# Weight sums in another order, and a chunk's last gate behind the next chunk's first PSUM copy, in a four-layer trunk on one core

## The chip, the core and the metric

The kernel runs on one core of a Trainium2 chip. The metric is the device time of one execution in microseconds (us), as the median of several runs. The engines are TensorE (PE in the profile; PEld is its weight load), VectorE (DVE), ScalarE (ACT), GpSimd (POOL) and SyncE (SP, which issues the loads). Each takes its own instructions in order, and waits at an instruction until all that it needs is there.

## The reference, cut to what matters

A trunk of four layers over 256 rows of width 1024, all in fp32. Each layer is a feed-forward block (FFN), an attention (of one of three kinds) and another FFN, so there are eight FFNs. The change lies in the FFN alone.

```python
D_MODEL, SEQ, DEPTH, D_FF = 1024, 256, 4, 2816

def swiglu(x, w_in, w_out):
    gate, up = jnp.split(x @ w_in, 2, axis=-1)
    return (jax.nn.silu(gate) * up) @ w_out

for i in range(DEPTH):
    h = h + 0.5 * rms_norm(swiglu(rms_norm(h, g[0]), ffn_w_in[i, 0], ffn_w_out[i, 0]), g[1])
    m = ...  # one of three attentions of rms_norm(h, g[2])
    h = h + rms_norm(m, g[3])
    h = h + 0.5 * rms_norm(swiglu(rms_norm(h, g[4]), ffn_w_in[i, 1], ffn_w_out[i, 1]), g[5])
```

## The kernel before

**Products.** An fp32 product is made of three products of fp32r parts. Every weight unit of 1 MB (a "raw" tile of 128 x 2048) is split into hi, cast by ScalarE (L156), and lo = raw − hi, by VectorE (L157). A group for one unit is then 12 matmuls of 128x512 (L152): four steps of k, each hi·xh, lo·xh, hi·xl. At most RAWS = 9 raw buffers and UNITS = 4 split units are held at a time in an FFN, and the names b00, b01, ... below are such units.

**An FFN** goes over D_FF in six chunks: chunk 0 is 512 wide, chunk 1 is 256 wide, chunks 2 to 5 are 512 wide. Chunks 0 and 1 are "plain" (function plain): gate and up for the two row tiles of 128, one after the other. Chunks 2 to 5 are in WINO (function wino): the eight products of the gate and the up of two row tiles, each in two halves of k, are made from seven, after Winograd. With b00, b01 the gate's and the up's upper half of k, and b10, b11 the lower, the weights of the seven are b00, b10, t2 = b00 + b01 + b11, t1 = b00 + b01, t3 = b01 + b11, b11, and t4 = t2 + b10 in this order. The left sides are rows of x, or sums of them (sh, sl in the profile).

**Where the sums are made.** plan_wino lists the loads and the splits ("preps") of a chunk, and fill works them off while there are raw buffers and split slots free. After the split of b00, VectorE adds b01 to b00 (L372): that is t1. After the split of b10, VectorE makes t2 = t1 + b11 in a buffer of its own (L372), and a DMA issued by GpSimd adds b11 to b01 (L375): t3. After the split of t2, another such DMA adds b10 to t2 (L375): t4. So there are two VectorE sums and two adding DMAs in a chunk, 64 of each in the kernel.

**Through a chunk.** wino(j) fills PSUM bank pb with b00, copies it to sl0 on ScalarE (L487), transposes the gate of the chunk before for row tile 0 (turn, tpg, L434; the transposed gate is split to gh and gl with L156 and L157), fills bank pa with b10, adds it to sl0 (L482) and takes the silu (L493), transposes the gate for row tile 1, and adds t2 on top of b00 in pb. That is why the copy of pb must be over first. Then the chunk before goes through its down projection in pieces (y, L244 to L246), with the products of t1, t3, b11 and t4 in between. The two gates of a chunk are made with up (L426) on VectorE: gate 0 after b11, gate 1 at the end, after t4's product has been added to sl1 (L482) and sl1 has gone through the silu (L518).

**What sets the order.** The code only says in which order the work is written; a scheduler of the language then sets each engine's list from it, once, when the kernel is built. The numbered names in the lists below are the built program's: g01_3_1 is the gate of layer 0, FFN 1, chunk 3, row tile 1, and raw423 or lo446 are the numbers of a raw tile or a split unit.

Of the kernel before, what the change touches and what calls it, by code (L numbers as in the profile page):

```python
# [11 lines left out]
AF = mybir.ActivationFunctionType  # L12
ALU = mybir.AluOpType
# [33 lines left out]
class Trunk:  # L47
# [235 lines left out]
    def ffn(self, l, f, X, ahead, end):  # L283
        nc = self.nc
        with self.tc.tile_pool(name=f"ffn{l}{f}", bufs=2, reuse_waits="tile") as pool:
# [73 lines left out]
            def plan_wino(j):  # L359


                c0, w = chunks[j]
                name = lambda n: (j, n)
                quarter = lambda k, u: (w_in, k * 512, 4, u * D_FF + c0, w)
                c1, w1 = chunks[j - 1]
                ko = [((j - 1, "o", k), (w_out, c1 + k * P, 2, 0, D)) for k in range(0, w1 // P, 2)]
                for n, src in ((name("b00"), quarter(0, 0)), (name("b01"), quarter(0, 1)),
                               (name("b10"), quarter(1, 0)), (name("b11"), quarter(1, 1)), (name("t2"), None), *ko):
                    loads.append(lambda n=n, src=src: raw(n, src))

                def add(to, a, b):
                    nc.vector.tensor_tensor(R[name(to)], R[name(a)], R[name(b)], op=ALU.add)  # L372

                def add_by_dma(to, b):
                    nc.gpsimd.dma_start(R[name(to)], R[name(b)], accum_op=ALU.add)  # L375

                def quarters(n, then=()):
                    split(name(n), name(n))
                    for x in then:
                        (add if len(x) == 3 else add_by_dma)(*x)  # L380

                def last_of(n, of, gone=None):
                    split(name(n), name(of), True)
                    if gone:
                        free(name(gone))

                outs = [lambda n=n: split(n, n, True) for n, _ in ko]
                preps.extend([
                    lambda: quarters("b00", [("b00", "b00", "b01")]),
                    lambda: quarters("b10", [("t2", "b00", "b11"), ("b01", "b11")]),  # L390
                    lambda: quarters("t2", [("t2", "b10")]),
                    outs[0],
                    lambda: last_of("t1", "b00"),
                    lambda: last_of("t3", "b01"),
                    lambda: last_of("b11", "b11")])
                if j < last:
                    preps.extend(outs[1:])
                preps.append(lambda: last_of("t4", "t2", "b10"))
                if j == last:
                    preps.extend(outs[1:])  # L400

# [8 lines left out]
            def unit(n):  # L410
                fill()
                return U[n]
# [57 lines left out]
            def wino(j):  # L470
# [16 lines left out]
                nc.scalar.copy(sl0, B)  # L487
                fill()
# [12 lines left out]
                o(1, 0)  # L501
                times(B, s31, 4, "t1", False)
# [14 lines left out]
                add(sl1, C)  # L517
                nc.scalar.activation(sl1, sl1, AF.Silu, scale=X[1][1])  # L518
                up(1, g1, 512, sl1, j, nr[1], g1)
                fill()  # L520
                if j < last:
                    del G[j - 1, 0], G[j - 1, 1]

# [19 lines left out]
            zig = [(0, 0), (0, 1), (1, 0), (1, 1)]  # L543
            for j in range(1, last + 1):
                if j in WINO:
                    wino(j)
                    continue
                plain(j, zig, [lambda: turn(j - 1, 0), lambda: turn(j - 1, 1)])
# [5 lines left out]
                del G[j - 1, 0], G[j - 1, 1]  # L554
            turn(last, 0)
# [770 lines left out]
```

## Time and profile before

| | us |
|---|---|
| median of 3 runs | 2004.0 (2003.55 to 2004.16) |
| the profiled execution | 2004.23 |
| its span in the profile | 2002.3 |
| TensorE busy | 1932.5 (97%) |
| VectorE busy | 1609.4 (80%) |
| ScalarE busy | 1257.2 (63%) |
| GpSimd busy | 188.6 (9%) |

The profile is of one execution; times in its views count from the span's start. TensorE's granted clock was 0.998 of full speed on average. A row of a timeline says when an instruction started, how long it took, its engine, line and operation, the tiles that it writes and reads, and, in square brackets, how long the engine had been idle before it and what ended that. A matmul's duration is longer than the distance to the next one, since they are pipelined.

### The profile page before, as it was taken

The numbers are of one execution on the slowest core, as the hardware profiler recorded it, in microseconds if no ns is written. First come the engines' busy times: TensorE is split into PE (matmuls) and PEld (weight loads), VectorE is DVE, ScalarE is ACT, GpSimd is POOL, SyncE is SP. The second block draws the span as 40 slices with busy tenths as digits, with TensorE's granted clock in tenths as the row PEclk, the third lists the DMA queues.
The fourth block names the chain that finished last, engine by engine and source line by source line (L and its number), as shares of the span: only waits on it lengthen the run. The fifth ranks groups of instructions, "written<-read, shape, count | busy, mean of one in ns | idle before, by whom it ended". The sixth has DMA issues, their size and how long they took to land.

```text
span 2002.3 us, 25733 instructions
## 1 busy us (share of the span) xinstructions
PE 1932.5 (97%) x9712; PEld 1584.9 (79%) x9712; DVE 1609.4 (80%) x2040; ACT 1257.2 (63%) x1721; POOL 188.6 (9%) x303
## 2 busy tenths in 40 slices
PE   7999999999999999999999999999999999999998
PEld 6777878777877878877887787678778777878776
DVE  6888678888788766788879877877988888678886
ACT  6566666566566566566656666865666657576654
POOL 0001210000000120000000032000000000210000
PEclk9999999999999999999999999999999999999999
DMA  9795638696787556687877675166868785638782
GB/s 360 213 295 140 211 120 294 184 294 188 245 274 222 169 189 212 184 278 211 283 221 212 209 205 165 60 242 200 230 208 300 202 286 148 206 105 286 203 286 55
DMA packets 177867, 430.25 MB, mean 215 GB/s; under 512 B 8784, under 2 KB 37712, under 8 KB 169552
## 3 DMA queue, kind: packets, MB, share of 16 engines
q1 hardware_dynamic: 168528, 361.51, 50.7%
q0 software_dynamic: 9216, 67.11, 17.6%
q8 instruction: 76, 1.25, 0.2%
q14 instruction: 47, 0.39, 0.1%
HBM read 360.43 MB, written 1.05 MB: 181 GB/s over the span
## 4 chain that ended last, share of the span: by engine, by line
PE 79%; ACT 8%; DVE 7%; issue 3%; POOL 0%; ACTq 0%; DVEq 0%; POOLq 0%
PE ps L152 13%; PE pb L152 12%; PE y L246 9%; PE y L244 9%; PE y L245 9%; PE pc L152 6%; ACT hi L156 5%; PE pa L152 4%; PE pw L670 4%; PE pw L672 4%; PE pw L671 3%; DVE lo L157 3%; DVE raw L372 2%; PE tpg L434 1%; ACT gh L156 1%
## 5 line engine op out<-in xcount | busy, mean ns | idle before, releaser
L157 DVE TENSOR_TENSOR lo<-raw,hi 128x2048 fp32r<-128x2048 f32 (+3 forms) x534 | 984.7, 1861 | 251.3 <-ACT hi L156 250.8
L156 ACT CAST hi<-raw 128x2048 fp32r<-128x2048 f32 (+3 forms) x534 | 824.8, 1563 | 481.6 <-DVE raw L372 189.9
L244 PE MATMUL y<-hi,gh 128*128 128x512 f32 x704 | 277.6, 394 | 5.1 <-ACT gh L156 5.1
L245 PE MATMUL y<-lo,gh 128*128 128x512 f32 x704 | 275.2, 391 | 0.0
L246 PE MATMUL y<-hi,gl 128*128 128x512 f32 x704 | 265.7, 391 | 0.0
L152 PE MATMUL ps<-hi,xh 128*128 128x256 f32 (+1 forms) x512 | 175.4, 342 | 1.9 <-ACT xh L156 1.3
L152 PE MATMUL pb<-hi,sh 128*128 128x512 f32 x384 | 153.1, 399 | 21.1 <-ACT sl L487 21.1
L152 PE MATMUL ps<-lo,xh 128*128 128x256 f32 (+1 forms) x512 | 173.2, 338 | 0.2 <-DVE lo L157 0.2
L152 PE MATMUL ps<-hi,xl 128*128 128x256 f32 (+1 forms) x512 | 172.9, 338 | 0.0
L244 PEld LDWEIGHTS y<-hi,gh 128*128 128x128 f32 x704 | 132.2, 188 | 41.7 <-ACT gh L156 15.2
L670 PE MATMUL pw<-hi,xh 128*128 128x512 f32 (+2 forms) x432 | 164.6, 381 | 0.0
L672 PE MATMUL pw<-hi,xl 128*128 128x512 f32 (+2 forms) x432 | 155.9, 361 | 0.0
L671 PE MATMUL pw<-lo,xh 128*128 128x512 f32 (+2 forms) x432 | 155.4, 360 | 0.0
L246 PEld LDWEIGHTS y<-hi,gl 128*128 128x128 f32 x704 | 132.2, 188 | 27.4
L375 POOL DMA_DIRECT2D raw<-raw x64 | 55.5, 868 | 1037.6 <-DVE raw L372 644.3
L245 PEld LDWEIGHTS y<-lo,gh 128*128 128x128 f32 x704 | 132.3, 188 | 26.0
L152 PE MATMUL pb<-lo,sh 128*128 128x512 f32 x384 | 151.8, 395 | 0.0
L152 PE MATMUL pb<-hi,sl 128*128 128x512 f32 x384 | 149.5, 389 | 0.0
L372 DVE TENSOR_TENSOR raw<-raw,raw 128x2048 f32<-128x2048 f32 x64 | 146.0, 2282 | 0.0
L152 PEld LDWEIGHTS ps<-hi,xh 128*128 128x128 f32 x512 | 97.6, 191 | 13.2 <-ACT xh L156 2.2
L152 PEld LDWEIGHTS pb<-hi,sh 128*128 128x128 f32 x384 | 72.0, 188 | 45.3 <-ACT sl L487 31.2
L152 PEld LDWEIGHTS ps<-lo,xh 128*128 128x128 f32 x512 | 97.6, 191 | 11.2 <-DVE lo L157 1.1
(213 smaller groups left out, 3327.2 us busy)
## 6 DMA issues: line engine op xcount, KB each, us to landing
raw<-in_ffn_w_in SPq DMA_DIRECT2D x172, 1024.0 KB, 8.4
raw<-in_ffn_w_out SPq DMA_DIRECT2D x88, 1024.0 KB, 9.2
raw<-raw POOLq DMA_DIRECT2D x64, 1024.0 KB, 7.0
raw<-in_diff_w_in SPq DMA_DIRECT2D x24, 1024.0 KB, 5.2
raw<-in_moba_w_in SPq DMA_DIRECT2D x12, 1024.0 KB, 5.2
raw<-in_nsa_w_in SPq DMA_DIRECT2D x9, 1024.0 KB, 5.1
raw<-in_diff_w_out SPq DMA_DIRECT2D x8, 1024.0 KB, 4.9
gpre<-in_norm_g SPq DMA_DIRECT2D x12, 512.0 KB, 5.9
```

The lines of the kernel that those rows point to most:

```text
L152: nc.tensor.matmul(out, l, r, start=first and i == 0, stop=last and i == len(steps) - 1, skip_group_check=more)
L156: self.nc.scalar.copy(hi, src)
L157: self.nc.vector.tensor_tensor(lo, src, hi.bitcast(F32), op=ALU.subtract)
L244: nc.tensor.matmul(y[b], x[0][:, kt, :], hi[:, k, s], start=f, stop=False)
L245: nc.tensor.matmul(y[b], x[0][:, kt, :], lo[:, k, s], start=False, stop=False)
L246: nc.tensor.matmul(y[b], x[1][:, kt, :], hi[:, k, s], start=False, stop=l)
L372: nc.vector.tensor_tensor(R[name(to)], R[name(a)], R[name(b)], op=ALU.add)
L375: nc.gpsimd.dma_start(R[name(to)], R[name(b)], accum_op=ALU.add)
L434: nc.tensor.transpose(tp[:, k, :], g[:, k * P:(k + 1) * P], self.ident)
L670: nc.tensor.matmul(out, x[0][:, kt, :], hi[:, k, :], start=first and i == 0, stop=False)
L671: nc.tensor.matmul(out, x[0][:, kt, :], lo[:, k, :], start=False, stop=False)
L672: nc.tensor.matmul(out, x[1][:, kt, :], hi[:, k, :], start=False, stop=last and i == len(todo) - 1)
```

## The change

In wino chunks the weight sums are made in another order:

- t1 gets a buffer of its own. t1 = b00 + b01 is a VectorE sum (L406), and b01 += b11, which is t3, an adding DMA (L407). Both stand in a new function sums_of(j + 1), which is called one chunk ahead: in wino(j) after the first down-projection pieces, for chunk 2 inside plain(1). It first takes loads off the list until t1 has its buffer.
- In the chunk itself, after the split of b10, VectorE adds b01 to b00 (L374). As b01 is b01 + b11 by then, that is t2. After the split of t2 the adding DMA b00 += b10 makes t4 (L378).
- The loads are listed as b00, b01, b11, (t1's buffer), b10, then the units of the down projection. In the last chunk the remaining units of the down projection still come after t4.
- The number of sums, adding DMAs, loads, splits and products is as before.

The last gate of a chunk (the add to sl1, the silu and up) becomes a function gate1 that wino returns. It is called in the next chunk's wino, behind the copy of pb to sl0, and after the last chunk at the end. unit calls fill only where the unit isn't there yet.

```diff
-                for n, src in ((name("b00"), quarter(0, 0)), (name("b01"), quarter(0, 1)),
-                               (name("b10"), quarter(1, 0)), (name("b11"), quarter(1, 1)), (name("t2"), None), *ko):
+                for n, src in ((name("b00"), quarter(0, 0)), (name("b01"), quarter(0, 1)), (name("b11"), quarter(1, 1)),
+                               (name("t1"), None), (name("b10"), quarter(1, 0)), *ko):
                     loads.append(lambda n=n, src=src: raw(n, src))
...
+                def sum_t2():
+                    split(name("b10"), name("b10"))
+                    nc.vector.tensor_tensor(R[name("b00")], R[name("b00")], R[name("b01")], op=ALU.add)
+
+                def split_t2():
+                    split(name("t2"), name("b00"))
+                    nc.gpsimd.dma_start(R[name("b00")], R[name("b10")], accum_op=ALU.add)
+
+                def split_t4():
+                    split(name("t4"), name("b00"), True)
+                    free(name("b10"))
 
                 outs = [lambda n=n: split(n, n, True) for n, _ in ko]
                 preps.extend([
-                    lambda: quarters("b00", [("b00", "b00", "b01")]),
-                    lambda: quarters("b10", [("t2", "b00", "b11"), ("b01", "b11")]),
-                    lambda: quarters("t2", [("t2", "b10")]),
+                    lambda: split(name("b00"), name("b00")),
+                    sum_t2,
+                    split_t2,
                     outs[0],
-                    lambda: last_of("t1", "b00"),
-                    lambda: last_of("t3", "b01"),
-                    lambda: last_of("b11", "b11")])
+                    lambda: split(name("t1"), name("t1"), True),
+                    lambda: split(name("t3"), name("b01"), True),
+                    lambda: split(name("b11"), name("b11"), True)])
...
+            def sums_of(j):
+
+                if j not in WINO:
+                    return
+                while (j, "t1") not in R:
+                    loads.pop(0)()
+                b01 = R[j, "b01"]
+                nc.vector.tensor_tensor(R[j, "t1"], R[j, "b00"], b01, op=ALU.add)
+                nc.gpsimd.dma_start(b01, R[j, "b11"], accum_op=ALU.add)
...
             def unit(n):
-                fill()
+                if n not in U:
+                    fill()
                 return U[n]
...
                 nc.scalar.copy(sl0, B)
+                gate1()
                 fill()
                 turn(j - 1, 0)
...
                 o(0, 0)
                 o(1, 0)
+                sums_of(j + 1)
                 times(B, s31, 4, "t1", False)
...
                 times(C, X[1][0], 4, "t4", False)
-                add(sl1, C)
-                nc.scalar.activation(sl1, sl1, AF.Silu, scale=X[1][1])
-                up(1, g1, 512, sl1, j, nr[1], g1)
-                fill()
+
+                def gate1():
+                    add(sl1, C)
+                    nc.scalar.activation(sl1, sl1, AF.Silu, scale=X[1][1])
+                    up(1, g1, 512, sl1, j, nr[1], g1)
                 if j < last:
                     del G[j - 1, 0], G[j - 1, 1]
+                return gate1
...
-                plain(j, zig, [lambda: turn(j - 1, 0), lambda: turn(j - 1, 1)])
+                plain(j, zig, [lambda: turn(j - 1, 0), lambda: turn(j - 1, 1), lambda: sums_of(j + 1)])
...
+            gate1()
+            fill()
             turn(last, 0)
```

**In the built lists.** First VectorE at the end of chunk 3 of the second FFN. Before: lo445 is the split of chunk 4's b00, lo446 that of its b10, lo447 that of its t2.

```order
L157 TENSOR_TENSOR lo445_3579<-raw423_3350,hi445_3578 128x2048
L426 SCALAR_TENSOR_TENSOR g01_3_0_3595<-pb431_3433,st396_3004,sl01_3_0_3446 128x512
L372 TENSOR_TENSOR raw423_3350<-raw423_3350,raw424_3352 128x2048
L157 TENSOR_TENSOR lo446_3598<-raw430_3431,hi446_3597 128x2048
L372 TENSOR_TENSOR raw436_3482<-raw423_3350,raw433_3452 128x2048
L482 TENSOR_TENSOR sl01_3_1_3504<-pc444_3564,sl01_3_1_3504 128x512
L157 TENSOR_TENSOR lo447_3628<-raw436_3482,hi447_3627 128x2048
L426 SCALAR_TENSOR_TENSOR g01_3_1_3554<-g01_3_1_3554,st397_3006,sl01_3_1_3504 128x512
```

After, with the rows ahead of it (lo437, lo439 and lo441 are splits of chunk 3's b11, of an output unit and of t4; g01_3_1 at L490 is the add of a product to the last gate's up part):

```order
L157 TENSOR_TENSOR lo437_3507<-raw402_3045,hi437_3506 128x2048
L406 TENSOR_TENSOR raw433_3452<-raw423_3350,raw424_3352 128x2048
L157 TENSOR_TENSOR lo439_3537<-raw421_3320,hi439_3536 128x2048
L157 TENSOR_TENSOR lo441_3559<-raw395_2990,hi441_3558 128x2048
L490 TENSOR_TENSOR g01_3_1_3556<-pc444_3566,g01_3_1_3556 128x512
L157 TENSOR_TENSOR lo445_3581<-raw423_3350,hi445_3580 128x2048
L434 SCALAR_TENSOR_TENSOR g01_3_0_3596<-pb429_3424,st396_3004,sl01_3_0_3437 128x512
L157 TENSOR_TENSOR lo446_3599<-raw436_3481,hi446_3598 128x2048
L374 TENSOR_TENSOR raw423_3350<-raw423_3350,raw424_3352 128x2048
L490 TENSOR_TENSOR sl01_3_1_3504<-pc444_3566,sl01_3_1_3504 128x512
L157 TENSOR_TENSOR lo447_3628<-raw423_3350,hi447_3627 128x2048
L434 SCALAR_TENSOR_TENSOR g01_3_1_3556<-g01_3_1_3556,st397_3006,sl01_3_1_3504 128x512
```

One sum (L406) now stands three splits, an add and a gate earlier, and between the two gates there are two splits and one sum instead of two splits and two sums.

Second, ScalarE in the same stretch. Before: hi447 is the cast of t2, L518 the last gate's silu, hi448 and hi451 the casts of an output unit and of chunk 4's t1, L487 the copy of pb.

```order
L156 CAST hi447_3627<-raw436_3482 128x2048
L518 ACTIVATE sl01_3_1_3504<-sl01_3_1_3504,st368_2826 128x512
L156 CAST hi448_3647<-raw438_3510 128x2048
L487 COPY sl01_4_0_3666<-pb450_3653 128x512
L156 CAST hi451_3668<-raw423_3350 128x2048
L156 CAST gh01_3_0_3679<-tpg01_3_0_3674 128x512
```

After:

```order
L156 CAST hi447_3627<-raw423_3350 128x2048
L530 ACTIVATE sl01_3_1_3504<-sl01_3_1_3504,st368_2826 128x512
L495 COPY sl01_4_0_3657<-pb448_3644 128x512
L156 CAST hi449_3662<-raw438_3510 128x2048
L156 CAST hi451_3668<-raw433_3452 128x2048
L156 CAST gh01_3_0_3678<-tpg01_3_0_3673 128x512
```

The copy stands one cast earlier; the cast of t2 and the silu are still ahead of it.

Third, VectorE at the end of chunk 2. Before: lo422 is the split of chunk 2's t4, lo425 and lo427 those of chunk 3's b00 and b10.

```order
L157 TENSOR_TENSOR lo422_3347<-raw386_2881,hi422_3346 128x2048
L157 TENSOR_TENSOR lo425_3369<-raw395_2990,hi425_3368 128x2048
L482 TENSOR_TENSOR g01_2_1_3366<-pc426_3373,g01_2_1_3366 128x512
L372 TENSOR_TENSOR raw395_2990<-raw395_2990,raw400_3039 128x2048
L157 TENSOR_TENSOR lo427_3388<-raw402_3045,hi427_3387 128x2048
L372 TENSOR_TENSOR raw416_3266<-raw395_2990,raw413_3245 128x2048
L426 SCALAR_TENSOR_TENSOR g01_2_0_3405<-pb414_3247,st396_3004,sl01_2_0_3260 128x512
L482 TENSOR_TENSOR sl01_2_1_3314<-pc426_3373,sl01_2_1_3314 128x512
```

After (raw413, the buffer of chunk 3's t1, takes the place in memory that raw378, which lo422 reads, leaves):

```order
L157 TENSOR_TENSOR lo422_3347<-raw378_2849,hi422_3346 128x2048
L406 TENSOR_TENSOR raw413_3245<-raw395_2990,raw400_3039 128x2048
L157 TENSOR_TENSOR lo425_3371<-raw395_2990,hi425_3370 128x2048
L490 TENSOR_TENSOR g01_2_1_3368<-pc426_3374,g01_2_1_3368 128x512
L157 TENSOR_TENSOR lo427_3389<-raw416_3265,hi427_3388 128x2048
L434 SCALAR_TENSOR_TENSOR g01_2_0_3405<-pb414_3246,st396_3004,sl01_2_0_3259 128x512
L374 TENSOR_TENSOR raw395_2990<-raw395_2990,raw400_3039 128x2048
L490 TENSOR_TENSOR sl01_2_1_3314<-pc426_3374,sl01_2_1_3314 128x512
```

The sum for t1 stands one split and one add ahead of where it was, right behind the split of chunk 2's t4, and gate 0 now stands ahead of the sum that makes t2.

## Rows read from the trace of the kernel before

**Rows 1.** The page's head: the span, and each engine's busy time

```profile
span 2002.3 us, 25733 instructions
...
PE 1932.5 (97%) x9712; PEld 1584.9 (79%) x9712; DVE 1609.4 (80%) x2040; ACT 1257.2 (63%) x1721; POOL 188.6 (9%) x303
```

**Rows 2.** TensorE's waits: line, releaser; us in total, times, longest us

```profile
PE pb L152 <- ACT sl L487: 21.1, 24, 0.9
PE tpg L434 <- DVE g L426: 14.1, 8, 1.8
...
PE y L244 <- ACT gh L156: 5.1, 24, 0.2
...
PE ps L152 <- DVE lo L157: 0.2, 1, 0.2
```

**Rows 3.** Timeline of TensorE, chunk 3 to 4: start us, us, instruction [idle before]

```profile
423.63 0.39 PE L152 MATMUL pb<-lo,xh 128*128 128x512 f32 x1
423.86 0.40 PE L152 MATMUL pb<-hi,xl 128*128 128x512 f32 x1
...
427.05 0.39 PE L152 MATMUL pa<-hi,xl 128*128 128x512 f32 x1
428.34 0.51 PE L152 MATMUL pb<-hi,sh 128*128 128x512 f32 x1 [0.90 <-ACT sl L487]
...
432.33 0.39 PE L245 MATMUL y<-lo,gh 128*128 128x512 f32 x1
432.93 0.50 PE L244 MATMUL y<-hi,gh 128*128 128x512 f32 x1 [0.21 <-ACT gh L156]
```

**Rows 4.** Timeline of ScalarE in the passages 2 to 3 and 3 to 4

```profile
395.18 0.57 ACT L487 COPY sl<-pb 128x512 f32<-128x512 f32 x1
...
423.49 1.90 ACT L156 CAST hi<-raw 128x2048 fp32r<-128x2048 f32 x1 [8.16 <-DVE raw L372]
425.30 0.72 ACT L518 ACTIVATE sl<-sl,st 128x512 f32<-128x512 f32 x1
425.92 1.89 ACT L156 CAST hi<-raw 128x2048 fp32r<-128x2048 f32 x1
427.71 0.57 ACT L487 COPY sl<-pb 128x512 f32<-128x512 f32 x1
```

**Rows 5.** Timeline of VectorE, chunk 3 to 4

```profile
408.82 2.29 DVE L157 TENSOR_TENSOR lo<-raw,hi 128x2048 fp32r<-128x2048 f32 x1 [2.39 <-ACT hi L156]
...
416.03 0.74 DVE L426 SCALAR_TENSOR_TENSOR g<-pb,st,sl 128x512 f32<-128x512 f32 x1
...
418.89 2.28 DVE L157 TENSOR_TENSOR lo<-raw,hi 128x2048 fp32r<-128x2048 f32 x1
...
425.42 2.29 DVE L157 TENSOR_TENSOR lo<-raw,hi 128x2048 fp32r<-128x2048 f32 x1 [1.44 <-ACT hi L156]
427.63 0.75 DVE L426 SCALAR_TENSOR_TENSOR g<-g,st,sl 128x512 f32<-128x512 f32 x1
```

**Rows 6.** Timeline of VectorE, chunk 2 to 3

```profile
378.18 2.29 DVE L157 TENSOR_TENSOR lo<-raw,hi 128x2048 fp32r<-128x2048 f32 x1 [2.29 <-ACT hi L156]
381.34 2.29 DVE L157 TENSOR_TENSOR lo<-raw,hi 128x2048 fp32r<-128x2048 f32 x1 [0.87 <-ACT hi L156]
...
384.15 2.28 DVE L372 TENSOR_TENSOR raw<-raw,raw 128x2048 f32<-128x2048 f32 x1
...
390.75 0.74 DVE L426 SCALAR_TENSOR_TENSOR g<-pb,st,sl 128x512 f32<-128x512 f32 x1
```

**Rows 7.** Timeline of TensorE, chunk 2 to 3

```profile
391.55 0.66 PE L434 MATMUL tpg<-ident,g 128*128 128x128 f32 x4 [1.76 <-DVE g L426]
...
399.09 0.39 PE L244 MATMUL y<-hi,gh 128*128 128x512 f32 x1
```

**Rows 8.** The adding DMAs of L375: one issue on GpSimd, and all landings

```profile
386.79 0.85 POOL L375 DMA_DIRECT2D raw<-raw  x1 [21.94 <-DVE raw L372]
...
DMA to landing us min/median/max: 6.9/7.0/9.7
```

More of the change, by code (lines that the diff above doesn't have):

```diff
@@ L369, in plan_wino @@
                     loads.append(lambda n=n, src=src: raw(n, src))
[L371 to L385, printed above, removed]
+                def sum_t2():
[4 more added lines that the diff above has]
+                    nc.gpsimd.dma_start(R[name("b00")], R[name("b10")], accum_op=ALU.add)
@@ L392, in plan_wino @@
                     outs[0],
-                    lambda: last_of("t1", "b00"),
-                    lambda: last_of("t3", "b01"),
-                    lambda: last_of("b11", "b11")])
+                    lambda: split(name("t1"), name("t1"), True),
+                    lambda: split(name("t3"), name("b01"), True),
+                    lambda: split(name("b11"), name("b11"), True)])
                 if j < last:
                     preps.extend(outs[1:])
-                preps.append(lambda: last_of("t4", "t2", "b10"))
+                preps.append(split_t4)
@@ L468, in plain, with wino @@
                         between.pop(0)()
-            def wino(j):
+            def wino(j, gate1):
                 def times(ps, x, at, n, first):
@@ L543, in ffn @@
             zig = [(0, 0), (0, 1), (1, 0), (1, 1)]
+            gate1 = lambda: None
             for j in range(1, last + 1):
                 if j in WINO:
-                    wino(j)
+                    gate1 = wino(j, gate1)
                     continue
-                plain(j, zig, [lambda: turn(j - 1, 0), lambda: turn(j - 1, 1)])
+                plain(j, zig, [lambda: turn(j - 1, 0), lambda: turn(j - 1, 1), lambda: sums_of(j + 1)])
                 for t in range(NT):
```

## The prediction

> **What bounds the kernel now.** I read the page's head first: TensorE is busy for 1932.5 us of a span of 2002.3 us [rows 1], so nothing can be won except in the 70 us in which it stands still, or by taking products away, and the change takes none away. So the second view is TensorE's own waits [rows 2]. Two of its lines come from the place that is edited: 24 waits for the copy of a PSUM bank (sl, L487), 21.1 us in all, and 8 waits of the transposes for a gate (g, L426), 14.1 us in all. A third, 24 waits for gh, 5.1 us, stands some 5 us behind the first in the program. 24 is three in each of the eight feed-forward blocks (FFNs): the passages from chunk 2 to 3, 3 to 4 and 4 to 5. 8 is one in each FFN, and it is the passage 2 to 3. The second FFN stands below for all.
>
> Third, the timelines there, TensorE first. In the passage 3 to 4 one product follows another after 0.23 us (423.63, 423.86), but the first product with t2 starts 1.29 us after the last of the group before it (427.05, 428.34) [rows 3]: 1.06 us lost. Its duration of 0.51 instead of 0.40 adds 0.11. The gh wait (432.33 to 432.93) loses 0.37 in the same way and 0.11 again, so 1.65 us go in one passage.
>
> Why the copy is late is read on ScalarE [rows 4]: the bank that it copies is complete at 423.86 + 0.40 = 424.26 [rows 3], but the copy starts at 427.71. ScalarE runs its list in order, and ahead of the copy stand the cast of t2 (423.49, after 8.16 us of waiting for a VectorE sum), the silu of the last gate and another cast. VectorE [rows 5] shows where the 8.16 us come from: behind the first gate (416.03) come a sum, a split (418.89), the second sum, and only then the cast of t2 can start; t2's split waits 1.44 us for it. The same view shows VectorE idle for 2.39 us ahead of 408.82. So a sum is on the path at the chunk's end while there is an unused hole as long as a sum 15 us before.
>
> **The change part by part.** *Sums and DMAs.* Per chunk there are still two VectorE sums and two adding DMAs; splits and loads are the same in number. No engine gets less work; all of the effect is order.
>
> *Passages 3 to 4 and 4 to 5.* The sum b00 + b01 for the next chunk moves into the hole ahead of 408.82: a sum takes 2.28 us [rows 6], the hole 2.39 [rows 5], so it costs nothing there as long as the hole is that long. Behind the first gate one sum is left. In the clock of before: gate 416.03 and about 0.66; split of b10 416.7 to 418.9; the sum t2 418.9 to 421.1 (2.2 us from start to start, 425.42 to 427.63 [rows 5]); cast of t2 421.1 to 423.0 (1.90 [rows 4]), instead of 423.49 to 425.3; silu to 423.7; the copy now stands right behind the silu, and starts at 424.3, when its bank is complete, instead of 427.71. The split of t2 ends at 425.3 and the last gate at 426.0. TensorE wants the copy's bank and the gate at 427.05 + 0.23 = 427.28 [rows 3]. Both are there, by 2.4 and 1.3 us, so the wait goes. What is late next is gh: ScalarE's list goes on from 424.9 instead of 428.2, so gh is ready near 431.4, and TensorE, now 1.2 us earlier, wants it at about that time. This wait shrinks to between nothing and what it was. The gain in a passage is 1.17 to 1.65 us; I take 1.55, near the upper end, since ScalarE is 3.4 us earlier and TensorE only 1.2. For 16 passages: 24.8 us (18.7 to 26.4).
>
> The adding DMA b01 + b11 has a reader on this path, the sum t2 (L374), which takes it from the same buffer. It is issued when the moved sum ends, near 408.7 and 0.36 (a sum at 384.15 for 2.28, its DMA at 386.79 [rows 6, 8]), and lands 6.9 to 9.7 us later, median 7.0 [rows 8]: 416 to 418.8, and it is wanted at 418.9. It fits.
>
> *Passage 2 to 3.* Here it does not fit. In the built program, t1 of chunk 3 gets the buffer that t4 of chunk 2 leaves, and the split that leaves it starts at 378.18 [rows 6]. So the moved sum runs from 380.4 to 382.6, and the split of b00 (before at 381.34) is pushed to 382.6 to 384.8. Then add, split of b10 and the first gate: 388.4, against 390.75 and 0.7 before, so the 1.76 us that the transposes wait [rows 7] go. But now L374 has to wait for the DMA: 382.6 + 0.36 + 7.5 = 390.5. I take 7.5 and not the median of 7.0, because weight loads are in flight here at that time. L374 ends at 392.8, the cast at 394.7, the split of t2 at 396.95, the gate at 397.65. Queued behind L374 on VectorE are the add to sl, the split of gh, the split of t2 and the last gate; TensorE's second t2 product (397.0) and its transposes (397.65) wait for the last two. Ten more products bring the first y product to 400.0, against 399.09 before [rows 7]: 0.9 later, less 0.48 for a gh wait that goes. Net loss 0.4 in a passage (a gain of 0.1 at a landing of 7.0, a loss of 1.1 at 8.2), for eight: 3.4 us (a gain of 0.8 to a loss of 9).
>
> *The rest.* In the first two chunks the sums for chunk 2 run ahead under plain products. At the end of an FFN the last gate has nothing to move behind, and the last two out units change places with t4. I cost both at nothing: TensorE waited only 0.2 us for a VectorE split in the plain groups [rows 2]. If that cover is gone, it costs at most one sum in an FFN, 8 × 2.28 = 18 us. A gain there is excluded, since there is no wait to remove.
>
> *Sum.* Against the profiled run's 2004.2 (0.2 above the median of the three runs): 2004.2 − 24.8 + 3.4 = 1982.8 us, so 1983. With the ends of the two terms: 1977 to 1994.
>
> **The rivals.** *A, slower: the DMA decides.* A landing that is d later than 7.5 us moves t2 by d at once in the passage 2 to 3, and in the other two from about d = 1.9 on. An FFN then gains 2.7 − d − 2·max(0, d − 1.9). This turns negative at d = 2.2, a landing of about 9.7 us, and at d = 3 it is −2.5, in all 2024 us. For it: all these DMAs are now issued while loads are running, and L374 cannot start without one. Against it: the median of 64 is 7.0 and 9.7 is the longest [rows 8].
>
> *B, no gain: VectorE becomes the bound.* Nine splits and two sums at 2.2 and seven small steps (adds, gates, splits of gh) of some 0.6 us are 28.5 us of VectorE in a chunk, and the chunk is to shrink from 32.5 us (the copies at 395.18 and 427.71 [rows 4]) to 31. The hole of 2.39 shrinks when TensorE gets faster, since it ends with casts that wait for slots freed by TensorE. If t2's split comes 1.9 us later than in my walk, TensorE's second t2 product waits for it, and from there the gain goes one to one; at 3.4 us nothing of 24.8 is left, and the passage 2 to 3 still loses: 2007. Half of that is 1995. For it: few idle moments are left. Against it: the two idle stretches of rows 5 together are 3.8 us, more than the 1.6 that the chunk loses.
>
> *C, the cover in the plain chunks or at the end is gone:* up to 18 of the 21 us are given back, 1983 to 2001.
>
> *D, faster still: a short landing.* If the DMA landed before VectorE comes to L374 at 388.4, t2's cast would start at 391.2, behind the cast of gh, its split end at 395.4, the gate at 396.1 and the first y product at 398.4 instead of 399.09: 0.7 and 0.48 gained in eight passages instead of 0.4 lost, 9 us, and 2004.2 − 24.8 − 9 = 1970. This needs a landing under 5.4 us; none of 64 was under 6.9 [rows 8]. The Trainium skill ("DMA: Bandwidth & Descriptors", section "Anatomy of one DMA — SWDGE (gpsimd) path") gives 2.0 us plus the bytes over 436 GB/s for a DMA issued by GpSimd, 4.4 us for 1 MB, and by that D would be the forecast. The trace does not agree: its adding DMAs of 1 MB take 7.0.
>
> *E: the edit does not do what it says.* The built order has the copy right behind the silu and one sum behind the first gate, so only other waits could undo it; that is A to C.
>
> **How the numbers follow.** The forecast has 0.60 (1977 to 1994), A 0.13, B 0.13, C 0.08, D 0.06. The predicted time is 1983 us. The range of 1972 to 2004 holds the forecast, most of C and of D and the better half of B; it leaves out A and the rest of B. About 0.2% is what a measurement of this kernel can tell from no change, 4 us here. Faster by more: the forecast, C and D nearly whole, and half of B, 0.77. Within: the rest of B and a little of A and C, 0.09. Slower: most of A and a part of B, 0.14.
>
> **What would show it.** In TensorE's waits of the changed kernel the 24 waits for the sl copy should be gone or be 8, and those of the transposes for g much under 14.1 us; in their place 8 waits for hi or lo of t2, some 2 to 4 us each, in the passage 2 to 3 alone. VectorE's L374 should be idle for about 2 us in that passage, released by a DMA, and not in the other two. The distance between the copies of chunks 3, 4 and 5 should fall from 32.5 to about 31. I am wrong if t2 is waited for in all three passages (B or A, told apart by what releases L374), or if the plain products wait for splits.

## The result, and the profile after

The change makes the kernel slower: 2028.6 us (median of four runs, 2027.2 to 2030.2) against 2004.1 us, a ratio of 1.0122 with a 95% interval of 1.0105 to 1.0140. The profiled execution has a span of 2026.1 us instead of 2002.3 [rows 1], 23.8 us more. The prediction was 1983 us with a range of 1972 to 2004, and its rival A (the adding DMA decides) was put at 2024.

The page's head of the changed kernel has:

```profile
span 2026.1 us, 25676 instructions
...
PE 1951.0 (96%) x9712; PEld 1600.6 (79%) x9712; DVE 1614.9 (80%) x2040; ACT 1258.4 (62%) x1721; POOL 187.6 (9%) x303
```

TensorE has the same 9712 instructions, but 18.5 us more of busy time: its granted clock is 0.988 on average instead of 0.998. Its waits (line, releaser; us in total, times, longest us) answer to [rows 2]:

```profile
PE pb L152 <- ACT hi L156: 18.8, 8, 4.2
PE pb L152 <- DVE lo L157: 18.6, 16, 1.8
...
PE tpg L442 <- DVE g L434: 6.1, 8, 1.3
...
PE y L244 <- ACT gh L156: 1.5, 9, 0.2
```

The 24 waits for the sl copy (21.1 us) are gone, and so are the 8 gate waits of 14.1 us in the passage 2 to 3. The 8 gate waits of 6.1 us are new ones, seven of them in the passage 4 to 5 and one in 3 to 4, and gh costs 1.5 us instead of 5.1. TensorE now waits for hi and lo of a weight unit. Eight of the 16 lo waits are 0.51 us each, for the split of b00; the other eight and the eight hi waits are all for t2, in the passage from chunk 2 to chunk 3.

VectorE's waits for the landing that L374 needs are

```profile
DVE raw L374 <- DMA raw<-raw: 49.8, 19, 8.4
```

Of these 26.4 us stand in the eight sums of chunk 3, 13.4 in those of chunk 5, 1.6 in those of chunk 4, and 8.4 in one sum, chunk 2 of the first FFN.

The sums from passage to passage come from the first down-projection product of each chunk in the two traces; the difference between two such points, added over the eight FFNs, is 36.9 us lost in the passage 2 to 3, 11.5 won in 3 to 4, 5.4 in 4 to 5 and 1.4 in the last chunk. Another 5.2 us are lost between the FFNs and at the ends. 36.9 − 11.5 − 5.4 − 1.4 + 5.2 = 23.8.

The passage 2 to 3 of the second FFN runs 5.06 us later than before (the split of chunk 2's t4 starts at 383.24 instead of 378.18 [rows 6]). VectorE there, with the idle time before a row and what ended it in brackets:

```profile
383.24 2.29 DVE L157 TENSOR_TENSOR lo<-raw,hi 128x2048 fp32r<-128x2048 f32 x1 [2.30 <-ACT hi L156]
385.57 2.29 DVE L406 TENSOR_TENSOR raw<-raw,raw 128x2048 f32<-128x2048 f32 x1
387.78 2.28 DVE L157 TENSOR_TENSOR lo<-raw,hi 128x2048 fp32r<-128x2048 f32 x1
...
392.78 0.75 DVE L434 SCALAR_TENSOR_TENSOR g<-pb,st,sl 128x512 f32<-128x512 f32 x1
396.07 2.29 DVE L374 TENSOR_TENSOR raw<-raw,raw 128x2048 f32<-128x2048 f32 x1 [2.55 <-DMA raw<-raw]
...
400.39 2.29 DVE L157 TENSOR_TENSOR lo<-raw,hi 128x2048 fp32r<-128x2048 f32 x1 [0.82 <-ACT hi L156]
```

GpSimd issues the DMA behind the moved sum, and again for the next two chunks (timeline):

```profile
388.45 0.85 POOL L407 DMA_DIRECT2D raw<-raw  x1 [18.54 <-DVE raw L406]
...
416.03 0.85 POOL L407 DMA_DIRECT2D raw<-raw  x1 [11.90 <-DVE raw L406]
...
447.94 0.85 POOL L407 DMA_DIRECT2D raw<-raw  x1 [12.84 <-DMA raw<-in_ffn_w_in]
```

The view of that line, for its 32 DMAs, has

```profile
DMA to landing us min/median/max: 7.5/10.9/12.5
```

which answers to [rows 8], where the 64 of before took 6.9, 7.0 and 9.7. In the passage 4 to 5 of the same FFN the sum waits for its landing as well, and TensorE for the gate that stands behind the sum in VectorE's list:

```profile
459.82 2.29 DVE L374 TENSOR_TENSOR raw<-raw,raw 128x2048 f32<-128x2048 f32 x1 [1.98 <-DMA raw<-raw]
467.17 0.66 PE L442 MATMUL tpg<-ident,g 128*128 128x128 f32 x4 [0.95 <-DVE g L434]
```

TensorE in the passage 2 to 3:

```profile
398.46 0.39 PE L152 MATMUL pa<-hi,xl 128*128 128x512 f32 x1
400.41 0.50 PE L152 MATMUL pb<-hi,sh 128*128 128x512 f32 x1 [1.56 <-ACT hi L156]
402.74 0.50 PE L152 MATMUL pb<-lo,sh 128*128 128x512 f32 x1 [1.82 <-DVE lo L157]
...
403.78 1.05 PE L442 MATMUL tpg<-ident,g 128*128 128x128 f32 x4
...
405.06 0.63 PE L152 MATMUL pb<-hi,sl 128*128 128x512 f32 x1
405.49 0.63 PE L152 MATMUL pb<-hi,sh 128*128 128x512 f32 x1
...
407.41 0.39 PE L244 MATMUL y<-hi,gh 128*128 128x512 f32 x1
```

Between the product of 398.46 and that of 402.74 TensorE makes a single one, at 400.41. Behind that standstill the products come 0.43 us apart (405.06, 405.49) instead of 0.23 [rows 3], with nothing to wait for. The stretches show why (us; PE, PEld, DVE, ACT and POOL busy; granted clock; DMA share; GB/s):

```profile
398.00:400.40 2.40, 0.85 (x4) 0.38 (x2) 1.58 (x4) 1.94 (x2) 0.00 (x0) 1.00 0.00 0
400.40:403.70 3.30, 1.47 (x4) 0.85 (x5) 3.30 (x3) 3.30 (x3) 0.43 (x1) 0.93 0.00 0
403.70:405.00 1.30, 1.30 (x6) 1.18 (x5) 1.30 (x1) 1.30 (x2) 0.43 (x1) 0.50 0.50 101
405.00:406.00 1.00, 1.00 (x4) 0.74 (x3) 1.00 (x2) 1.00 (x1) 0.00 (x0) 0.50 0.93 188
406.00:407.30 1.30, 1.30 (x6) 1.07 (x5) 1.30 (x1) 0.85 (x2) 0.00 (x0) 0.76 1.02 195
407.30:411.00 3.70, 3.70 (x18) 3.05 (x17) 3.70 (x4) 3.01 (x3) 0.00 (x0) 1.00 0.95 154
```

The granted clock is 0.50 for about three microseconds, the 1.2 GHz level, after TensorE had stood still twice, and it returns to 1.00, the 2.4 GHz level. The other FFNs show the same in this passage, some of them for longer (in the first, 0.50 from 101 to 106.2).

### The profile page after: what moved, and what is told of

Same layout as the page of the kernel before. It is cut to its first block, busy times and chain, and to the rows that moved or that the text cites. A ratio compares the mean times of both kernels' runs of the same rounds, so it can differ in the third digit from the quotient of the medians.

```text
span 2026.1 us, 25676 instructions
## 1 busy us (share of the span) xinstructions
PE 1951.0 (96%) x9712; PEld 1600.6 (79%) x9712; DVE 1614.9 (80%) x2040; ACT 1258.4 (62%) x1721; POOL 187.6 (9%) x303
## 3 DMA queue, kind: packets, MB, share of 16 engines
q0 software_dynamic: 9216, 67.11, 17.7%
HBM read 360.43 MB, written 1.05 MB: 178 GB/s over the span
## 4 chain that ended last, share of the span: by engine, by line
PE 65%; issue 14%; ACT 7%; DVE 7%; DMA 6%; POOL 1%; POOLq 0%; SPq 0%; DVEq 0%; ACTq 0%
PE pb L152 12%; PE y L246 7%; PE y L244 7%; PE y L245 7%; PE pc L152 6%; PE ps L152 6%; ACT hi L156 4%; PE pw L685 4%; PE pw L687 3%; PE pw L686 3%; DMA raw<-raw 3%; DMA raw<-in_ffn_w_in 3%; DVE lo L157 3%; PE pa L152 2%; PE tpg L442 1%
## 5 line engine op out<-in xcount | busy, mean ns | idle before, releaser
L152 PE MATMUL pb<-hi,sh 128*128 128x512 f32 x384 | 157.6, 410 | 18.8 <-ACT hi L156 18.8
L152 PE MATMUL pb<-lo,sh 128*128 128x512 f32 x384 | 157.5, 410 | 14.5 <-DVE lo L157 14.5
L152 PE MATMUL pb<-hi,sl 128*128 128x512 f32 x384 | 155.5, 405 | 0.0
L374 DVE TENSOR_TENSOR raw<-raw,raw 128x2048 f32<-128x2048 f32 x32 | 73.3, 2289 | 49.8 <-DMA raw<-raw 49.8
L152 PEld LDWEIGHTS ps<-hi,xl 128*128 128x128 f32 x512 | 97.6, 191 | 11.1 <-DVE xl L157 1.1
## 6 DMA issues: line engine op xcount, KB each, us to landing
raw<-in_ffn_w_out SPq DMA_DIRECT2D x88, 1024.0 KB, 11.1
```

The lines of the kernel that those rows point to most:

```text
L152: nc.tensor.matmul(out, l, r, start=first and i == 0, stop=last and i == len(steps) - 1, skip_group_check=more)
L374: nc.vector.tensor_tensor(R[name("b00")], R[name("b00")], R[name("b01")], op=ALU.add)
```

## The experiments

Theory L says that the loss is the landing of the adding DMA L407, which VectorE's L374 has to wait for, and with it the clock. The rivals: S, the moved sum and the new order of splits and loads are the loss; G, the moved gate is; K, the clock falls for a reason of its own. L2 is a later form of L: the landings for chunks 4 and 5 are too late as well. Each run's ratio is to the kernel before, which took 2003.9 to 2004.3 us beside it.

**t2 without the DMA's result, in all chunks.** The edit on the changed kernel:

```diff
-                    nc.vector.tensor_tensor(R[name("b00")], R[name("b00")], R[name("b01")], op=ALU.add)
+                    nc.vector.tensor_tensor(R[name("b00")], R[name("b00")], R[name("b11")], op=ALU.add)
```

> The changed kernel, but the VectorE sum L374 adds b11 and not b01 to b00, so that it no longer waits for the adding DMA L407; t2 is then b00 + b11, which leaves a part of t2 out. Sums, DMAs, splits, loads and products stay the same in number and place. Theory L (the landing of L407 is the loss: VectorE waits for it in the passage 2 to 3, TensorE stands still behind it and its clock falls): the waits of TensorE for hi and lo of t2 go in all passages, the granted clock is again above 0.995, and the time falls from 2028.6 to between 1970 and 1985 us. Rival S (the loss is the moved sum L406 ahead of the split of b00, and the other order of loads): only the wait goes that VectorE shows, the time stays above 2010.

Measured: 1971.5 us (ratio 0.9836, 0.9822 to 0.9851), granted clock 0.999. TensorE's first waits in the FFNs are now

```profile
PE pc L152 <- ACT hi L156: 8.6, 8, 1.1
...
PE pb L152 <- DVE lo L157: 4.1, 8, 0.5
```

so all waits for t2 are gone, and only the split of b00 still delays it by 0.5 us in each FFN. Order, counts and buffers are those of the changed kernel, so 57 us hang on this one wait. S falls: what is left of the moved sum's delay are these 4.1 us.

**Chunk 3 alone, and chunks 4 and 5 alone.** The same edit, for chunk 3 only, and in the other kernel with (4, 5) in place of (3,):

```diff
-                    nc.vector.tensor_tensor(R[name("b00")], R[name("b00")], R[name("b01")], op=ALU.add)
+                    nc.vector.tensor_tensor(R[name("b00")], R[name("b00")], R[name("b11" if j in (3,) else "b01")], op=ALU.add)
```

> The changed kernel, with L374 of chunk 3 alone adding b11 in place of b01 (so t2 of chunk 3 leaves out b01, and that sum waits for no DMA); chunks 2, 4 and 5 are as in the changed kernel. Theory L in its first form (only the passage 2 to 3 has a landing too late): nearly all of the 57 us that go when no chunk waits, 1972 to 1985 us. Theory L2 (the landings of 10 to 12 us of the DMAs for chunks 4 and 5, issued among weight loads, are too late as well, which only shows where the passage 2 to 3 is quick): 1995 to 2010 us, with new waits of TensorE in the passages 3 to 4 and 4 to 5.

> The counterpart: L374 of chunks 4 and 5 alone adds b11 in place of b01; chunk 3 waits for its DMA as in the changed kernel. Theory L in its first form: hardly any change, 2022 to 2029 us. Theory L2: the waits of the last passage go, the passage 2 to 3 keeps its 37 us: 2008 to 2022 us.

Measured: 1997.4 us (0.9968, 0.9956 to 0.9980) without the wait in chunk 3, and 2008.2 us (1.0025, 1.0015 to 1.0034) without it in chunks 4 and 5. So the waits cost 31.2 and 20.4 us, together 51.6 of the 57; the wait of chunk 2 in the first FFN is left in both, and the remaining 5.5 us were not told apart. L in its first form falls and L2 stands: the last two passages lose too. In the first of the two kernels TensorE's waits begin with

```profile
PE y L246 <- DVE gl L157: 14.9, 17, 1.1
```

and VectorE's have

```profile
DVE raw L374 <- DMA raw<-raw: 32.9, 17, 8.3
```

The y products of the later chunks wait for gl, which stands behind L374 in VectorE's list. By the sums from passage to passage, the passages 3 to 4 and 4 to 5 together gain only 1.3 us in this kernel, against 16.9 in the changed one. There the passage 2 to 3 runs late, which leaves the DMA for chunk 4 more time (L374 of chunk 4 waits 1.6 us in all, here 11.0). For chunk 5 it does not: 13.4 us there, 13.6 here. That wait is behind the new gate waits of the changed kernel. In the second of the two kernels, where chunks 4 and 5 wait for nothing, TensorE's waits have no line for a gate or for gh, and the passage 4 to 5 gains 13.4 us instead of 5.4.

**Chunk 3 as before.** On the changed kernel, chunk 3 gets the old loads, sums and preps:

```diff
+OLD = (3,)
...
+                if j in OLD:
+                    preps.extend([
+                        lambda: quarters("b00", [("b00", "b00", "b01")]),
+                        lambda: quarters("b10", [("t2", "b00", "b11"), ("b01", "b11")]),
+                        lambda: quarters("t2", [("t2", "b10")]),
...
-                if j not in WINO:
+                if j not in WINO or j in OLD:
                     return
```

> The changed kernel, with chunk 3 of each FFN alone as in the kernel before (t1 in place, t2 in its own buffer, both sums in the chunk, loads in the old order); the moved gate and the new order stay in chunks 2, 4 and 5. Theory L: the passage 2 to 3 costs what it did before or a little less, the other two keep their measured gains of 11.5 and 5.4 us, and what else was lost (about 4 us) stays: 1985 to 1995 us. If the loss came from the new order in general, or from the moved gate (rival G), the time stays above 2010.

Measured: 2009.1 us (1.0018, 1.0009 to 1.0028). The expectation missed by 14 us, and the profile says where: VectorE waits 36.5 us for landings, in chunks 2, 4 and 5 only, and TensorE has 17 waits for gl (16.1 us) and 14 for gates (17.7 us). The gains of the later passages did not stay, for the reason that the two kernels above show. This was the first sign of L2. At 2009.1 beside the 2010 above which the expectation put the other readings, the run decides nothing by itself.

**The two parts of the change alone.** The gate alone, on the kernel before:

```diff
                 nc.scalar.copy(sl0, B)
+                gate1()
                 fill()
```

> The kernel before with the moved gate alone (the last gate's add, silu and up behind the next chunk's copy to sl; unit fills only where needed). The built list has the copy right behind the cast of t2, ahead of the silu. Theory L: the gate's move is harmless and worth little, since t2 is still cast at the same time behind two sums: the 24 waits for the sl copy (21 us) go, but TensorE then waits for t2's split or for the last gate nearly as long: 1995 to 2006 us. Rival G (the moved gate causes the loss): 2015 us or more.

Measured: 2005.1 us, no difference (1.0003, 0.9994 to 1.0012). The 24 waits for the copy (21.1 us) and the 24 for gh (5.1) are gone, and one group of 24.1 us takes their place; the 8 waits for the gate stay as they were:

```profile
PE pc L152 <- ACT hi L156: 24.1, 24, 1.1
PE tpg L435 <- DVE g L427: 14.1, 8, 1.8
```

(The edit also has gate1 returned and unit fill only where needed, as in the change.) The new waits are at the product of t3, for a ScalarE cast, and not where the expectation had them, at t2 or the last gate. The sums alone, on the changed kernel:

```diff
                     up(1, g1, 512, sl1, j, nr[1], g1)
+                gate1()
+                fill()
```

(and the call behind the copy is taken out again, and unit fills as before)

> The new order of sums alone: the last gate stays at the end of its chunk, ahead of the next chunk's first PSUM copy, and unit fills as before. Theory L: the waits for t2 in the passage 2 to 3 stay, and in the other passages the copy to sl waits again behind the last gate's silu and a cast, but t2 is cast earlier, so part of the gain stays: 2025 to 2045 us. Rival G (the moved gate is the loss): at or below 2004.

Measured: 2025.6 us (1.0106, 1.0090 to 1.0123), with the same waits for t2 (18.3 and 18.2 us) and clock 0.988. So the new order of sums makes 21.6 of the 24.6 us. G falls.

**Work laid into the standstill.** On the changed kernel, chunk 3 of each FFN:

```diff
+                if j == 3:
+                    self.product(A, X[0][0], [(4, unit((j, "b10")))], True, True, more=True)
                 times(A, X[0][0], 4, "b10", True)
```

> The changed kernel, with the b10 product of chunk 3 computed twice into the same bank, one group of 12 more matmuls in each FFN (96 in all, 21.8 us of TensorE at full clock) just ahead of the wait for t2. Theory L with the clock as a consequence of the standstill: the group lies in the wait, the clock does not fall behind it, and the 16 us of slow matmuls in these passages go: 2010 to 2022 us, granted clock above 0.994. Rival K (the clock falls for another reason): the slow matmuls stay, and the time is 2028 to 2050.

Measured: 2022.7 us (1.0091, 1.0076 to 1.0106): 96 more products, and the kernel is 5.9 us faster than the changed one. The granted clock is 0.998 again. In the trace, products that follow without a wait but more than 0.30 us apart exceed their 0.227 us by 28.7 us in all, against 43.6 in the changed kernel and 28.0 in the kernel before, so nearly all of the slow stretches are gone. The time is 0.7 us above the range that L had, and the gain is smaller than those 15 us. TensorE's waits for hi and lo of a weight unit go from 37.4 to 5.6 us, but others grow, the gates from 6.1 and gl from 0.4:

```profile
PE tpg L442 <- DVE g L434: 18.7, 17, 2.5
PE y L246 <- DVE gl L157: 13.4, 15, 1.1
```

How much of the rest the added group itself takes, where it is longer than the wait, was not told apart. In the first two FFNs the clock still falls; in the second TensorE waits 2.5 us for a gate behind the group. In the other six it stays. K falls: the clock follows the standstill.

**The DMA freed from VectorE.** The DMA b01 += b11 needs only loaded weights if t1 is not made from b01 first. So t2 = b00 + b01 as in the changed kernel, and t1 = t2 − b11 afterwards:

```diff
                 def split_t2():
                     split(name("t2"), name("b00"))
-                    nc.gpsimd.dma_start(R[name("b00")], R[name("b10")], accum_op=ALU.add)
+                    nc.gpsimd.dma_start(R[name("b10")], R[name("b00")], accum_op=ALU.add)
+
+                def split_t1():
+                    nc.vector.tensor_tensor(R[name("t1")], R[name("b00")], R[name("b11")], op=ALU.subtract)
+                    split(name("t1"), name("t1"), True)
...
-                nc.vector.tensor_tensor(R[j, "t1"], R[j, "b00"], b01, op=ALU.add)
-                nc.gpsimd.dma_start(b01, R[j, "b11"], accum_op=ALU.add)
+                nc.gpsimd.dma_start(R[j, "b01"], R[j, "b11"], accum_op=ALU.add)
```

> The changed kernel with the adding DMA b01 += b11 freed from VectorE: nothing is summed ahead, so the DMA is issued when b01 and b11 have landed; t2 = b00 + b01 as in the changed kernel; t1 = t2 - b11 by VectorE into t1's buffer, off the path; t4 is added into b10 instead of b00. Two VectorE sums and two DMAs a chunk as before. Theory L: in the passage 2 to 3 the DMA, issued some 20 us earlier, has long landed, t2 is not waited for and the clock stays; in the later passages b11 lands only shortly before, so that the DMA comes 2 to 3 us earlier than in the changed kernel, with some waits left: 1960 to 1985 us. Rival S (order of splits and loads): above 2005.

Measured: 2007.9 us (1.0015, 1.0006 to 1.0025). In this kernel and the next, sums_of stood behind the product of t3, and in chunk 3 t2 came to be written ahead of its DMA, so t2 there leaves out b11 and waits for nothing. The time lies where the expectation had rival S, but VectorE's waits say that it is again a landing, now in the passage 3 to 4 of all eight FFNs:

```profile
DVE raw L374 <- issue: 41.6, 8, 6.6
```

GpSimd's issue there in the second FFN, and VectorE's sum:

```profile
408.94 0.85 POOL L409 DMA_DIRECT2D raw<-raw  x1 [18.92 <-DMA raw<-in_ffn_w_in]
```

```profile
421.12 2.29 DVE L374 TENSOR_TENSOR raw<-raw,raw 128x2048 f32<-128x2048 f32 x1 [5.21 <-issue]
```

The DMA is issued as soon as b11 is loaded, but lands only 12.1 us later, and L374 starts then (the idle time is put down to no releaser, but the landing, at 421.04, is the one that fits). L2 again. The granted clock is 0.990 in this run, and it now falls in the passage 3 to 4 (0.85 from 426 to 430 and 0.78 from 430 to 435), behind a wait of 3.5 us for a gate, and no longer in 2 to 3. So it follows the standstill to another passage, which speaks against K once more.

**The loads in another order as well.** b01 and b11 first:

```diff
-                for n, src in ((name("b00"), quarter(0, 0)), (name("b01"), quarter(0, 1)), (name("b11"), quarter(1, 1)),
+                for n, src in ((name("b01"), quarter(0, 1)), (name("b11"), quarter(1, 1)), (name("b00"), quarter(0, 0)),
```

> As the one before, with the loads listed b01, b11, b00 instead of b00, b01, b11, so that in the later passages too both ends of the adding DMA are there long before t2 is wanted. Theory L: no VectorE sum waits for a landing in any passage, whatever the landing takes: 1955 to 1975 us, a few us under the one before. If landings in the later passages do not matter, the two are the same within 3 us.

Measured: 1965.8 us (0.9809, 0.9793 to 0.9826), 42 us under the one before by the order of three loads. GpSimd now issues chunk 4's DMA at 376.17, and VectorE's sum in that passage follows the split ahead of it without a gap:

```profile
376.17 0.85 POOL L409 DMA_DIRECT2D raw<-raw  x1 [24.84 <-DMA raw<-in_ffn_w_in]
```

```profile
410.35 2.28 DVE L157 TENSOR_TENSOR lo<-raw,hi 128x2048 fp32r<-128x2048 f32 x1
412.54 2.29 DVE L374 TENSOR_TENSOR raw<-raw,raw 128x2048 f32<-128x2048 f32 x1
```

**The same with all sums whole.** sums_of goes back to its place behind the first down-projection pieces, ahead of t2's sum in every chunk:

```diff
                 o(1, 0)
+                sums_of(j + 1)
                 times(B, s31, 4, "t1", False)
```

> As the kernel with the loads listed b01, b11, b00 and the adding DMA freed from VectorE, but with the DMA written ahead of t2's sum in every chunk; in the run of that kernel the sum of chunk 3 was written ahead of its DMA, so that t2 there lacked b11 and waited for no DMA at all. Theory L2: the DMAs are issued 20 us or more before t2 is wanted, so the true sum waits no more than the incomplete one did: 1962 to 1972 us, granted clock above 0.997. If the DMA is still too late in chunk 3: 1980 us or more.

Measured: 1965.8 us (0.9810, 0.9794 to 0.9827), granted clock 0.998. This kernel computes all of the reference, and is 38 us faster than the kernel before. Its DMAs b01 += b11 are hardly quicker than those of the changed kernel:

```profile
DMA to landing us min/median/max: 7.0/9.9/13.9
```

but they are issued 19 to 38 us before the sum (chunk 3's at 344.68; 13.7 in chunk 2 of the first FFN), and none of the 32 sums waits for one. In the passage 2 to 3:

```profile
379.67 2.28 DVE L157 TENSOR_TENSOR lo<-raw,hi 128x2048 fp32r<-128x2048 f32 x1
381.87 2.28 DVE L375 TENSOR_TENSOR raw<-raw,raw 128x2048 f32<-128x2048 f32 x1
```

**And without the moved gate.** The edit of the sums alone, on the kernel just shown:

```diff
                     up(1, g1, 512, sl1, j, nr[1], g1)
+                gate1()
+                fill()
```

> The fastest kernel so far (adding DMA freed from VectorE and written ahead of t2's sum, loads b01, b11, b00) without the moved gate: the last gate at its chunk's end, the copy to sl behind its silu and one more cast. Theory L2: t2 is cast 2.4 us earlier than in the kernel before, so the copy is in time in the old place too, and the gate's move is worth nothing or up to 3 us either way: 1963 to 1970 us. If the gate's move carries the gain: 1980 us or more.

Measured: 1963.9 us (0.9797, 0.9781 to 0.9813), the fastest of all. Eight of the waits for the copy remain, small:

```profile
PE pb L152 <- ACT sl L500: 4.9, 8, 0.6
```

The gate's move is worth nothing once t2 comes early.

## Why the prediction was wrong, point by point

**What bounds the kernel** was read rightly: t2 comes late behind two VectorE sums, and the copy, the gate and gh wait for it. The kernels in which no sum waits for a landing and t2 comes early take 1964 to 1966 us, 38 to 40 us less than before, where these three waits were 40.3 us in all [rows 2].

**The order in the passage 2 to 3** came as walked. With 5.06 us taken off, the moved sum ran from 380.5 (380.4 in the walk), the split of b00 from 382.7 (382.6), the first gate was over at 388.5 (388.4), the DMA was issued at 383.4 (383.0) and L374 started at 391.0 (390.5).

**The step that failed first is what follows in that passage**, the term of 3.4 us, which was measured as 36.9 for all eight. Three things make the difference of 33.5:

- *The clock.* The walk moved the first y product by what t2 came late, at full speed. In the second FFN the rest of t2's products, from 402.74 to 407.41, took 4.7 us where the walk had 3.0, at a granted clock of 0.50. Added up as in the filler's paragraph, the slow products in these eight passages lose 16.5 us. This was no term of the sum at all. The kernel before gave no row of a standstill of 4 us in these passages: its longest waits there were 0.9 and 1.8 us [rows 2], and its clock was full there.
- *The landing.* 7.5 us was the shortest and not the middle: in the eight FFNs the landings for chunk 3 were 7.5, 7.7, 7.8, 8.0, 8.3, 8.5, 9.2 and 10.4 us, 7.5 us more in sum than 8 × 7.5. The range given for this term, up to a landing of 8.2, was too narrow; a landing of 9.7 was on record [rows 8].
- *The account.* The 0.48 us for gh, 3.8 in eight passages, fall behind the first y product, so they show in the next passage's difference. The remaining 5.7 us go in small delays, such as a duration of 0.50 instead of 0.39 behind each of the two waits and transposes of 1.05 us at the low clock (0.66 before [rows 7]); they were not told apart.

**The second failed step is "It fits"** for the passages 3 to 4 and 4 to 5: 24.8 us were forecast there and 16.9 measured, and most of these depended on the lost time ahead of them (1.3 us where the passage 2 to 3 did not wait). The prediction's own sign failed with it: L374 was to wait for a DMA in the passage 2 to 3 alone, and it waits in 4 to 5 in all eight FFNs. The step put these DMAs at a landing of 6.9 to 9.7 us, from DMAs that had been issued into quieter moments; measured were 10.8 to 12.5 in these passages. The kernel without the waits in chunks 4 and 5 is 20.4 us faster.

**Why the landings grew.** Counted in both traces by the weight loads in flight between issue and landing, the adding DMAs of before had none (22 of them, median 6.95 us), one (34, 8.0) or two (8, 8.2). In the changed kernel 14 had five, with 10.8 to 12.5 us. But the count alone does not tell the landing: eight DMAs of the changed kernel for t4 (L378) had three loads in flight and took 8.1 to 8.2 us. What the loads moved meanwhile fits better. The DMA queue of the loads, in the changed kernel between issue and landing of the three adding DMAs of the second FFN (388.45, 416.03 and 447.94), with 7.5, 10.9 and 11.8 us:

```profile
q1 hardware_dynamic: 119, 0.42, 14.2%
q1 hardware_dynamic: 694, 2.37, 56.5%
q1 hardware_dynamic: 711, 2.73, 59.6%
```

(packets, MB, share of 16 engines). Of before, 39 DMAs had less than 0.05 MB of loads beside them (median 6.95 us), and 20 had 0.25 to 0.30 MB (8.0 to 8.2). In the changed kernel the DMAs for chunk 3 had 0.4 to 1.4 MB, and all 16 for chunks 4 and 5 had 2.3 to 2.9. The kernel of 1965.8 us shows a second thing that makes a landing long. Its DMAs for chunk 5 took 11.1 to 13.9 us, five of them beside only 0.2 MB of loads, and each was issued while GpSimd's DMA for t4 was still on its way:

```profile
416.27 0.85 POOL L379 DMA_DIRECT2D raw<-raw  x1 [30.68 <-DMA raw<-in_ffn_w_in]
416.97 1.04 POOL L412 DMA_DIRECT2D raw<-raw  x1
```

In the changed kernel no two adding DMAs overlap, so there the loads are the likeliest reading; it was not tested by itself, with the same DMA at the same place and no loads.

**The rivals.** A named the cause, the landings, and it had 0.13. That its 2024, for landings of 7.5 + 3 us in all three passages, comes near 2028.6 is partly luck: in the passage 2 to 3, where the loss fell, the landings were only 0.9 us above 7.5 on average, and the clock, which A has not, made a large part; in the other two they were 3.3 to 5.0 us above, and these passages still gained. What spoke against it, the median of 7.0, came from DMAs in other places of the load traffic, and the argument for it (all these DMAs are now issued while loads are running) should have weighed more. B (VectorE becomes the bound) did not come: the kernel of 1965.8 us, with as many sums and splits, has VectorE busy for 1609.3 us. C did not come in the plain chunks; 5.2 us were lost between FFNs and at the ends. 1.9 of them are ahead of the sixth FFN, where the granted clock in the attention is 0.50 from 1246.5 to 1249.5; the kernel before has 1.00 at the same products (1232 to 1236). Why it falls there was not looked into. D did not come, since no landing was under 6.9. Its rule of the Trainium skill ("DMA: Bandwidth & Descriptors", section "Anatomy of one DMA — SWDGE (gpsimd) path") gives an estimate of 4.4 us for 1 MB. These runs speak against it as a time for an adding DMA on this core, with 6.9 to 13.9 us.

**The sum of the parts as measured:** the gate's move alone nothing (2005.1), the new order of sums alone +21.6 (2025.6), both +24.6. Inside the change, the waits for landings cost 57 us, and what it brings without them is 32.5 (1971.5).

## What to carry to other kernels

A sum that moves to a DMA's result moves its reader behind a landing: price that DMA with the loads that will be in flight at its new place, not with the median of the old ones, and see whether it can be issued from loaded data alone, as here with t1 = t2 − b11 and the two loads that it needs listed first, which made 1964 to 1966 us of 2028.6. Where a wait of a few microseconds on the engine that bounds the kernel is new, put a row for the clock behind it into the sum. And moving a waiting instruction, as the gate here, buys nothing while the thing that all of them wait for comes no earlier.

## What the runs showed of the hardware

An adding DMA of 1 MB within the core's memory took 6.9 to 7.0 us in most cases without load traffic, 7.9 to 8.2 beside 0.25 to 0.30 MB of loads, and, in the changed kernel, 10.8 to 12.5 beside 2.3 to 2.9 MB. Issued while another adding DMA was on its way, it took 11.1 to 11.9 us beside 0.2 MB of loads. Two waits of TensorE of 1.56 and 1.82 us with one product between them were followed by a granted clock of 0.50 for some 3 us. In eight such passages, some with longer waits, the low clock lost half as much as the waits themselves (16.5 us beside 33.3). Single waits of 0.9 and 1.8 us in the same passages of the kernel before were not followed by a fall. With 12 more products ahead of each such pair of waits the granted clock of the whole run was 0.998 instead of 0.988, and the run was faster by 5.9 us.
